# A three-FFN network in split fp32: operand tiles and weights at varied SBUF places, and two other orders of the matmuls

## The chip, the cores and the metric

One Trainium2 chip, one core. The metric is device time in microseconds (us) of one execution of the whole program; lower is better.

## The reference

A sequence of 512 tokens of width 1024 goes through three layers, each a mixer and a gated FFN with a width-3 causal convolution:

```python
x = x + rms_norm(mix, g);  u = h @ w_up                    # 1024 -> 2*4096
u = conv_b + sum(conv_w[j] * u_pad[:, j:j + S] for j in range(3))
gate, val = jnp.split(u, 2, axis=-1)
x = x + rms_norm((gelu(gate) * val) @ w_down, g)           # 4096 -> 1024
...
def conv_ffn(h, w_in, conv_w, conv_b, w_out):              # twice, 1024 -> 2*2816 -> 1024
    u = h @ w_in
    ...
    g, v = jnp.split(u, 2, axis=-1)
    return (jax.nn.silu(g) * v) @ w_out
```

The mixers are, in turn, sliding-window attention with an RWKV-7 time mix, forgetting with differential attention, and a top-k sparse attention with stick-breaking attention. All inputs and outputs are fp32.

## The kernel before, in words

**Layout.** Activations stand transposed: 128 rows of one 128-wide slice of the width, 512 tokens along the free axis, 2048 B a tile. A product in fp32 is made of three fp32r products: an operand x is split into `hi` (x rounded to fp32r) and `lo` (the rest), a weight likewise into `wh` and `wl`, and `denses` (L213 to L224) adds wh\*hi (L222), wh\*lo (L223) and wl\*hi (L224) into one PSUM bank, for each of the k-steps (128 rows of the contraction each). Every matmul loads its own 128x128 weights (LDWEIGHTS, PEld in the profile). An output slice of an up projection takes 8 k-steps, so 24 matmuls of 512 columns.

**Weights.** A `Stream` fetches units of 8 weight tiles (512 KB) from HBM by SP's DMA queue into `raw` (3 buffers, L306). `unit` (L322) copies `raw` to `wh` on ACT (L335) and subtracts on DVE to give `wl` (L336). `wh` and `wl` have 2 buffers each of 4096 B, in the pool `w`. `take` gives the next tile of the unit.

**FFN** (`ffn`, L247). After two outputs ahead (`ahead`, L233), for each of nf column blocks f it makes two outputs one after the other, gate and value: `proj` fills a bank, DVE multiplies it by the norm's factor into `u` (L265), ACT and DVE apply the convolution (L266 to L268), ACT the activation (L271), POOL the product `zu` (L273), and `split` gives `gh` and `gl` (L130, L131). There are two chunks of blocks (16 and 16 in the 1st FFN, 11 and 11 in the 2nd and 3rd). After each chunk the down projection runs over the chunk's `gh`, `gl`: 8 outputs of 16 or 11 k-steps. In the last chunk of the 1st and 3rd FFN the down projection runs in two halves of 256 columns. The PSUM banks come from `psq` (L98): two banks `q` and one `b` in turn.

**Places.** SBUF pools lie one behind the other: constants `cst`, `xp` (`x`, `hh`, `hl`, 8 tiles each, `nsq`, `bc`), `w` (`raw`, `wh`, `wl`), the later constants `cst2`, and the pool of the running phase (`gh`, `gl` and others). All tiles of `xp` and `w` are multiples of 512 B, so `hh`, `hl` and every weight tile start at the same place within 512 B (byte 224). `cst2` holds 6720 B (13\*512 + 64), so `gh` and `gl` start 64 B further on in the 1st FFN; in the 2nd and 3rd 320 B of small tiles stand ahead of them too, which puts them 128 B lower (byte 96). `hh` and `hl` are the operand tiles of all projections but the down ones.

**Order of the work.** The code emits instructions in the order in which it reads. A list scheduler then fixes the order on each engine when the program is built: at each step an engine takes the earliest emitted of those instructions that its model of the times holds to be ready, and a tile that waits for a free buffer isn't ready. On the chip each engine runs its own list in that order and waits at semaphores.

Of the kernel before, what the change touches and what calls it, by code (L numbers as in the profile page):

```python
# [10 lines left out]
F32 = mybir.dt.float32  # L11
F32R = mybir.dt.float32r
# [10 lines left out]
P = 128  # L23
S = 512
# [12 lines left out]
FFN2 = dict(nf=22, chunks=((0, 11), (11, 22)))  # L37

F1 = {"z": 4, "za": 2, "zu": 2, "u": 3, "gh": 16, "gl": 16, "acc": 8}
F2 = {"z": 4, "za": 2, "zu": 2, "u": 3, "gh": 13, "gl": 13, "acc": 8}  # L40
M2 = {"ot": 7, "cT": 4, "aq": 2, "ak": 2, "avt": 2, "p": 4, "pT": 3, "PT": 4, "on": 2, "pre": 2}
M3 = {"ot": 4, "pre": 2, "rtmp": 1, "isc": 3, "irl": 2, "selb": 3, "kf": 4, "vd": 4, "PT": 3,
      "sq": 1, "sk": 1, "svt": 2, "e": 4, "sg": 2, "sc": 2, "cq": 4, "w3": 3}

GLOBAL = {"x": 8, "hh": 8, "hl": 8, "nsq": 2, "bc": 1}

BANKS = dict(q=2, s=2, b=1, n=1, a=1, o=1)

# [17 lines left out]
class K:  # L66
    def __init__(self, tc, ctx, dbg):
        self.tc, self.nc, self.dbg = tc, tc.nc, dbg or {}
        self.c = ctx.enter_context(tc.tile_pool(name="cst", bufs=1))
        self.xp = ctx.enter_context(tc.tile_pool(name="xp", bufs=1))  # L70
        self.w = ctx.enter_context(tc.tile_pool(name="w", bufs=1))
        self.ps = ctx.enter_context(tc.tile_pool(name="ps", bufs=1, space=PSUM))
        self.dr = ctx.enter_context(tc.tile_pool(name="dr", bufs=1, space=DRAM))
        self.n = self.nq = self.nt = 0
        self.spread = False

    @contextmanager
    def phase(self, name, bufs):
# [4 lines left out]
    def slot(self, name, shape=(P, S), dt=F32, tag=None):  # L83
        self.n += 1
        tag = tag or name
        if tag in GLOBAL:
            return self.xp.tile(list(shape), dt, name=f"{name}_{self.n}", tag=tag, bufs=GLOBAL[tag])
        return self.t.tile(list(shape), dt, name=f"{name}_{self.n}", tag=tag, bufs=self.bufs.get(tag, 1))
# [124 lines left out]
    def denses(self, qs, ws, rhs, cols=(0, S)):  # L213
        nc = self.nc
        c0, c1 = cols
        n = len(rhs)
        for k, (xh, xl) in enumerate(rhs):
            xh, xl = xh[:, c0:c1], xl[:, c0:c1]
            for q, w in zip(qs, ws):
                wh, wl = w.take() if isinstance(w, Stream) else w[k]  # L220
                o = q[:, c0:c1]
                nc.tensor.matmul(o, wh, xh, start=(k == 0), stop=False)  # L222
                nc.tensor.matmul(o, wh, xl, start=False, stop=False)  # L223
                nc.tensor.matmul(o, wl, xh, start=False, stop=(k == n - 1))  # L224

    def proj(self, st, rhs):
        if st.ready:
# [19 lines left out]
    def ffn(self, x, h, up, down, cw, nf, chunks, act, done, bc=None, parts=((0, S),), mid=None, before=None, after=None):  # L247
        nc = self.nc
        if bc is None:
            self.ahead(up, h, CFG["fa"])  # L250
            bc = self.rstd(x)
        acc = {}
        for ci, (f0, f1) in enumerate(chunks):
            if ci and mid:
                mid()
            g = []
            for f in range(f0, f1):
                z = []
                for part in range(2):
                    q = self.proj(up, h)  # L260
                    c = part * nf + f
                    col = lambda j: self.pv[:, cw + j * 2 * nf + c:cw + j * 2 * nf + c + 1]
                    y = self.slot("z")
                    v = self.slot("u")
                    nc.vector.tensor_tensor(v, q, bc, op=OP.mult)  # L265
                    nc.scalar.activation(y, v, AF.Identity, bias=col(3), scale=col(2))  # L266
                    nc.vector.scalar_tensor_tensor(y[:, 1:], v[:, :S - 1], col(1), y[:, 1:], op0=OP.mult, op1=OP.add)
                    nc.vector.scalar_tensor_tensor(y[:, 2:], v[:, :S - 2], col(0), y[:, 2:], op0=OP.mult, op1=OP.add)  # L268
                    z.append(y)
                a = self.slot("za")  # L270
                nc.scalar.activation(a, z[0], act)  # L271
                u = self.slot("zu")
                nc.gpsimd.tensor_tensor(u, a, z[1], op=OP.mult)  # L273
                g.append(self.split(u, "g"))
            if ci == len(chunks) - 1:
                i0 = down.i
                for i, cols in enumerate(parts):
                    if before:
                        before(i)
                    down.i = i0  # L280
                    for m in range(8):
                        q = self.psq()
                        self.denses([q], [down], g, cols)
                        done(m, q[:, cols[0]:cols[1]], acc[m][:, cols[0]:cols[1]], cols)
                    if after:
                        after(i, cols)
                break
            for m in range(8):
                q = self.psq()
                self.dense(q, down, g)  # L290
                if ci == 0:
                    acc[m] = self.slot("acc")
                    nc.scalar.activation(acc[m], q, AF.Copy)
                else:
                    nc.vector.tensor_tensor(acc[m], acc[m], q, op=OP.add)


class Stream:
# [23 lines left out]
    def unit(self, tags=None):  # L322
        k, nc = self.k, self.k.nc
        if self.raw is None:
            self.fetch()
        raw, self.raw = self.raw, None
        if tags:
            hi, lo = ([k.slot("xw", (P, 4, P), F32R, tag=t) for t in ts] for ts in (tags[:2], tags[2:]))
        else:
            hi = [k.w.tile([P, 8, P], F32R, name=f"wh_{k.n}", tag="wh", bufs=2)]  # L330
            lo = [k.w.tile([P, 8, P], F32R, name=f"wl_{k.n}", tag="wl", bufs=2)]
        n = 8 // len(hi)
        for i, (a, b) in enumerate(zip(hi, lo)):
            part = raw[:, i * n:(i + 1) * n]
            nc.scalar.activation(a, part, AF.Copy)  # L335
            (nc.gpsimd if self.pool > 0 else nc.vector).tensor_tensor(b, part, a.bitcast(F32), op=OP.subtract)  # L336
        self.pool -= 1
        return hi, lo
# [577 lines left out]
def rope_tables(k, I, tag):  # L916
    nc = k.nc
    k.caus = k.const("caus", I["c_caus"])
    k.causb = k.c.tile([P, P], BF16, name="causb")
    nc.vector.tensor_copy(k.causb, k.caus)  # L920
    k.tri = k.const("tri", I["c_tri"])
    k.strictb = k.c.tile([P, P], BF16, name="strictb")
    nc.vector.tensor_copy(k.strictb, k.const("strict", I["c_strict"]))
    pi, ang, n, t = (k.slot(name, dt=dt, tag=tag) for name, dt in (("pi", I32), ("ang", F32), ("nn", F32), ("rt", F32)))
    nc.sync.dma_start(pi, I["positions"].partition_broadcast(P))
    inv = k.const("invf", I["c_freq"])
    nc.vector.tensor_copy(ang, pi)
    nc.vector.tensor_scalar(ang, ang, inv[:, 0:1], None, op0=OP.mult)
    nc.vector.tensor_scalar(n, ang, 1.0 / (2 * math.pi), 12582912.0, op0=OP.mult, op1=OP.add)
    nc.vector.tensor_scalar(n, n, 12582912.0, None, op0=OP.subtract)  # L930
    for c in _two_pi():
        nc.vector.scalar_tensor_tensor(ang, n, -c, ang, op0=OP.mult, op1=OP.add)
    nc.vector.tensor_scalar(ang, ang, math.pi, -math.pi, op0=OP.min, op1=OP.max)
    k.cos, k.sin = k.c.tile([P, S], F32, name="cosT"), k.c.tile([P, S], F32, name="sinT")
    nc.scalar.activation(k.sin, ang, AF.Sin, scale=inv[:, 1:2])
    nc.scalar.activation(t, ang, AF.Abs)
    half = k.c.tile([P, 1], F32, name="halfpi")
    nc.gpsimd.memset(half, math.pi / 2)
    nc.scalar.activation(k.cos, t, AF.Sin, scale=-1.0, bias=half)
    k.rot = k.const("rot", I["c_rot"])  # L940


def _two_pi():
# [434 lines left out]
        f()  # L1378


@with_exitstack
def net(ctx, tc, I, out, dbg=None, stages=(1, 2, 3)):
    nc = tc.nc
    k = K(tc, ctx, dbg)
# [4 lines left out]
    nc.gpsimd.memset(k.ones, 1.0)  # L1389
    k.identb = k.c.tile([P, P], BF16, name="identb")  # L1390
    nc.vector.tensor_copy(k.identb, k.ident)
    if 1 in stages:
        x, h, st, bc, q = first_block(k, I, ctx)
    else:
# [6 lines left out]
    if 2 in stages:  # L1401
        with k.phase("m2", M2):
            even_layer(k, I, x, h, st, bc, q)
        with k.phase("f2", F2):
            ffn2(k, I, x, 0)
    if 3 in stages:
        with k.phase("m3", M3):
            odd_layer(k, I, x)
        with k.phase("f3", F2):
            ffn2(k, I, x, 1, out)  # L1410
    else:
        with k.phase("end", {"y": 3}):
            for m in range(8):
                nc.sync.dma_start(out[:, m], x[m])
# [144 lines left out]
```

## Time and profile before

| what | us |
|---|---|
| time, median of 2 runs (2328.59 to 2328.67) | 2328.63 |
| span of the profiled execution, first to last instruction | 2314.8 |
| time outside that span (difference of the two) | 13.8 |
| PE busy in the span | 2250.8 |
| DVE busy | 1429.2 |
| ACT busy | 924.8 |
| 1st FFN, up and down | 435 to 944 |
| 2nd FFN | 1260 to 1625 |
| 3rd FFN | 1934 to 2302 |

The FFN lines are times from the span's start, read off the matmuls of their projections. PE's busy time is that of modelled, pipelined matmuls that overlap one another (one lasts 0.39 us and the next starts after some 0.23), so the rate of the work is read from the starts of the matmuls and not from their lengths.

### The profile page before, as it was taken

To read this page: it belongs to the slowest core of one execution; us is meant where nothing else is said; L and a number is where in the kernel's file an instruction comes from. 1 tells how busy PE (TensorE), PEld (TensorE's weight loads), DVE (VectorE), ACT (ScalarE), POOL (GpSimd) and SP (SyncE) were. 2 spreads that over 40 slices of the span, in tenths; PEclk is the share of its full clock that TensorE was granted. 3 is DMA by queue.
4 is the path that set the end of the run, shared out by engine and by line. 5 is a ranking of instruction groups with operands and counts; after the bars stand their busy time and mean duration, and the time that the engine had idled before them with its cause. 6 is when DMAs were issued, how large, how long until landed. Compare 5 with 4: busy or idle time off the path is not lost.

```text
span 2314.8 us, 30327 instructions
## 1 busy us (share of the span) xinstructions
PE 2250.8 (97%) x11784; PEld 1768.7 (76%) x11784; DVE 1429.2 (62%) x2597; ACT 924.8 (40%) x1533; POOL 342.9 (15%) x325
## 2 busy tenths in 40 slices
PE   8899998999999999999999999999999999999998
PEld 6677677888888889966668888888656558888888
DVE  5978765766336666643675762664795656643665
ACT  4234433544334444333344442443243344433443
POOL 2111103311001113200011111111011201111111
PEclk9999998999999999999999999999999999999999
DMA  5111121233323245311112232323211102332334
GB/s 165 59 37 35 28 63 62 69 101 100 102 94 101 91 127 169 112 33 37 55 55 83 91 100 91 101 92 99 74 46 46 46 19 91 100 100 91 101 113 152
DMA packets 66305, 192.85 MB, mean 83 GB/s; under 512 B 15808, under 2 KB 19152, under 8 KB 66160
## 3 DMA queue, kind: packets, MB, share of 16 engines
q1 hardware_dynamic: 65584, 189.70, 26.1%
q0 software_dynamic: 576, 1.19, 0.3%
q8 instruction: 93, 1.52, 0.3%
q14 instruction: 52, 0.43, 0.1%
HBM read 188.24 MB, written 2.63 MB: 82 GB/s over the span
## 4 chain that ended last, share of the span: by engine, by line
PE 85%; DVE 9%; issue 2%; ACT 2%; POOL 2%; DMA 0%; SPq 0%; DVEq 0%; ACTq 0%; POOLq 0%
PE q L222 15%; PE q L224 15%; PE q L223 15%; PE b L222 7%; PE b L224 7%; PE b L223 7%; PE o L1011 2%; DVE wl L336 1%; DVE invm L650 1%; PE s L1326 1%; PE s L1129 1%; PE s L1168 1%; DVE sc L1307 1%; PE a L813 1%; POOL nsq L163 1%
## 5 line engine op out<-in xcount | busy, mean ns | idle before, releaser
L336 DVE TENSOR_TENSOR wl<-raw,wh 128x1024 fp32r<-128x1024 f32 x341 | 433.7, 1272 | 264.8 <-ACT wh L335 263.3
L335 ACT ACTIVATE wh<-raw 128x1024 fp32r<-128x1024 f32 x341 | 359.7, 1055 | 460.2 <-PE q L223 247.7
L222 PE MATMUL q<-hh,wh 128*128 128x512 f32 (+1 forms) x1294 | 511.3, 396 | 10.1 <-ACT hh L190 7.8
L224 PE MATMUL q<-hh,wl 128*128 128x512 f32 (+1 forms) x1294 | 511.1, 395 | 0.6 <-DVE wl L336 0.6
L223 PE MATMUL q<-hl,wh 128*128 128x512 f32 (+1 forms) x1294 | 509.2, 394 | 0.6 <-DVE hl L191 0.5
L222 PEld LDWEIGHTS q<-hh,wh 128*128 128x128 f32 x1294 | 246.2, 191 | 61.6 <-ACT hh L190 7.8
L223 PEld LDWEIGHTS q<-hl,wh 128*128 128x128 f32 x1294 | 246.3, 190 | 52.3 <-issue 5.4
L224 PEld LDWEIGHTS q<-hh,wl 128*128 128x128 f32 x1294 | 245.9, 190 | 52.3 <-issue 4.5
L223 PE MATMUL b<-hl,wh 128*128 128x512 f32 (+1 forms) x602 | 233.8, 388 | 0.0
L224 PE MATMUL b<-hh,wl 128*128 128x512 f32 (+1 forms) x602 | 231.9, 385 | 0.0
L222 PE MATMUL b<-hh,wh 128*128 128x512 f32 (+1 forms) x602 | 231.6, 385 | 0.0
L273 POOL TENSOR_TENSOR zu<-za,z 128x512 f32<-128x512 f32 x76 | 100.6, 1324 | 816.5 <-DVE z L268 759.7
L224 PE MATMUL q<-gh,wl 128*128 128x256 f32 (+1 forms) x559 | 189.5, 339 | 2.2 <-DVE wl L336 2.2
L222 PE MATMUL q<-gh,wh 128*128 128x256 f32 (+1 forms) x559 | 189.4, 339 | 1.7 <-ACT gh L130 1.0
L223 PE MATMUL q<-gl,wh 128*128 128x256 f32 (+1 forms) x559 | 188.5, 338 | 0.0
L130 ACT ACTIVATE gh<-zu 128x512 fp32r<-128x512 f32 x76 | 48.1, 632 | 250.6 <-POOL zu L273 250.5
L131 DVE TENSOR_TENSOR gl<-zu,gh 128x512 fp32r<-128x512 f32 x76 | 52.6, 692 | 150.9 <-ACT gh L130 150.7
L266 ACT ACTIVATE z<-u,pv 128x512 f32<-128x512 f32 x152 | 122.7, 810 | 31.2 <-DVE u L265 31.2
L163 POOL TENSOR_TENSOR nsq<-nsq,nsq 128x256 f32<-128x256 f32 (+1 forms) x84 | 96.7, 1153 | 245.1 <-ACT nsq L158 244.8
L223 PEld LDWEIGHTS b<-hl,wh 128*128 128x128 f32 x602 | 113.9, 189 | 23.3 <-issue 2.2
L224 PEld LDWEIGHTS b<-hh,wl 128*128 128x128 f32 x602 | 113.9, 189 | 23.1 <-issue 1.7
L222 PEld LDWEIGHTS b<-hh,wh 128*128 128x128 f32 x602 | 113.9, 189 | 22.3 <-issue 0.9
(554 smaller groups left out, 3455.0 us busy)
## 6 DMA issues: line engine op xcount, KB each, us to landing
raw<-in_ffn_up SPq DMA_DIRECT2D x88, 512.0 KB, 3.6
raw<-in_w_ffn_up SPq DMA_DIRECT2D x64, 512.0 KB, 3.6
raw<-in_ffn_down SPq DMA_DIRECT2D x55, 512.0 KB, 3.6
raw<-in_w_ffn_down SPq DMA_DIRECT2D x48, 512.0 KB, 3.6
raw<-in_ev_w_in SPq DMA_DIRECT2D x24, 512.0 KB, 3.6
raw<-in_w_in SPq DMA_DIRECT2D x20, 512.0 KB, 3.8
raw<-in_od_w_in SPq DMA_DIRECT2D x20, 512.0 KB, 3.6
x<-in_x SPq DMA_DIRECT2D x16, 256.0 KB, 4.1
```

Source lines behind the costliest of these rows:

```text
L130: nc.scalar.activation(hi, x, AF.Copy)
L131: nc.vector.tensor_tensor(lo, x, hi.bitcast(F32), op=OP.subtract)
L163: (nc.gpsimd if m % chains == 0 else nc.vector).tensor_tensor(acc, acc, sq, op=OP.add)
L222: nc.tensor.matmul(o, wh, xh, start=(k == 0), stop=False)
L223: nc.tensor.matmul(o, wh, xl, start=False, stop=False)
L224: nc.tensor.matmul(o, wl, xh, start=False, stop=(k == n - 1))
L266: nc.scalar.activation(y, v, AF.Identity, bias=col(3), scale=col(2))
L273: nc.gpsimd.tensor_tensor(u, a, z[1], op=OP.mult)
L335: nc.scalar.activation(a, part, AF.Copy)
L336: (nc.gpsimd if self.pool > 0 else nc.vector).tensor_tensor(b, part, a.bitcast(F32), op=OP.subtract)
L650: nc.vector.transpose(out=M[32 * g:32 * g + 32], in_=R[j]["aab"][32 * g:32 * g + 32, :, 32 * i:32 * i + 32] .rearrange("r u c -> r c u")[: ...
L1011: k.nc.tensor.matmul(o[64 * hh:64 * hh + 64, kb * P:], v(kb, hh), pts[hh][:, 4 * kb:3 * kb + NB].rearrange("p c t -> p (c t)"), start=(kb ...
```

## The change

`hh` and `hl` become eight tiles of 2304 B each, used in turn, with the operand at an offset of its own in each (`STARTS`, in bytes). `wh` and `wl` become two tiles of 4224 B with an offset for the even and the odd unit (`WSTARTS`). Two fillers and a smaller DMA scratch put the pools `xp`, `w` and the phase pool of the FFNs at multiples of 512 B. In the 2nd FFN the three products of a k-step run in the order wh\*hi, wl\*hi, wh\*lo. In the 3rd FFN gate and value of a block are made together: their matmuls alternate between two banks, and the weights have 3 buffers `wph`, `wpl` each in the phase pool, for the down projection of that FFN too.

```diff
-F2 = {"z": 4, "za": 2, "zu": 2, "u": 3, "gh": 13, "gl": 13, "acc": 8}
+F2 = {"wph": 3, "wpl": 3, "z": 4, "za": 2, "zu": 2, "u": 3, "gh": 13, "gl": 13, "acc": 8}
...
+STARTS = {"hh": (0, 16, 32, 48, 64, 128, 256, 192), "hl": (0, 0, 0, 0, 32, 32, 16, 16)}
+WSTARTS = ((0, 32), (0, 16))
...
     def slot(self, name, shape=(P, S), dt=F32, tag=None):
...
+        if tag in STARTS:
+            i = self.turn[tag] = (self.turn.get(tag, -1) + 1) % 8
+            t = self.xp.tile([P, 576], dt, name=f"{name}_{self.n}", tag=f"{tag}{i}")
+            return t[:, STARTS[tag][i] // 4:STARTS[tag][i] // 4 + S]
...
+        if self.paired and len(qs) == 2:
+            for k, (xh, xl) in enumerate(rhs):
+                us = [w[k] for w in ws]
+                for i, (a, x) in enumerate(((0, xh), (1, xh), (0, xl))):
+                    for q, u in zip(qs, us):
+                        nc.tensor.matmul(q[:, c0:c1], u[a], x[:, c0:c1], start=(k == 0 and i == 0), stop=(k == n - 1 and i == 2))
+            return
...
                 nc.tensor.matmul(o, wh, xh, start=(k == 0), stop=False)
-                nc.tensor.matmul(o, wh, xl, start=False, stop=False)
-                nc.tensor.matmul(o, wl, xh, start=False, stop=(k == n - 1))
+                for a, x, last in ((wl, xh, 0), (wh, xl, 1)) if self.swapped else ((wh, xl, 0), (wl, xh, 1)):
+                    nc.tensor.matmul(o, a, x, start=False, stop=(last == 1 and k == n - 1))
...
+                if self.paired:
+                    pair = up.ready[:2]
+                    del up.ready[:2]
+                    if not pair:
+                        pair = [self.psq(), self.psq()]
+                        self.denses(pair, [[up.take() for _ in range(8)] for _ in range(2)], h)
                 for part in range(2):
-                    q = self.proj(up, h)
+                    q = pair[part] if self.paired else self.proj(up, h)
...
-        if tags:
+        if k.paired:
+            hi, lo = ([k.slot(n, (P, 8, P), F32R)] for n in ("wph", "wpl"))
+        elif tags:
...
-            hi = [k.w.tile([P, 8, P], F32R, name=f"wh_{k.n}", tag="wh", bufs=2)]
-            lo = [k.w.tile([P, 8, P], F32R, name=f"wl_{k.n}", tag="wl", bufs=2)]
+            k.turn["w"] = i = 1 - k.turn.get("w", 1)
+            hi, lo = ([k.w.tile([P, 1056], F32R, name=f"{n}_{k.n}", tag=f"{n}{i}")[:, o[i] // 4:o[i] // 4 + 1024].rearrange("p (a b) -> p a b", b=P)]
+                      for n, o in zip(("wh", "wl"), WSTARTS))
...
+def filler(k, size):
+    k.n += 1
+    t = k.c.tile([P, size // 4], F32, name=f"filler_{k.n}")
+    k.nc.gpsimd.memset(t[:, 0:1], 0.0)
```

The fillers are called with 1824 (in `net`, ahead of the first block) and 1472 (at the end of `rope_tables`); `net` sets `k.swapped` around the 2nd FFN and `k.paired` from the 3rd on; the program is built with `dynamic_dma_scratch_size=8192`.

## Rows read from the trace of the kernel before

**Rows 1.** The page, part 1 and the clock line of part 2.

```profile
PE 2250.8 (97%) x11784; PEld 1768.7 (76%) x11784; DVE 1429.2 (62%) x2597; ACT 924.8 (40%) x1533; POOL 342.9 (15%) x325
...
PEclk9999998999999999999999999999999999999999
```

**Rows 2.** The page, part 4: the chain that ended last, by engine.

```profile
PE 85%; DVE 9%; issue 2%; ACT 2%; POOL 2%; DMA 0%; SPq 0%; DVEq 0%; ACTq 0%; POOLq 0%
```

**Rows 3.** Groups by line and shape, PE: count, busy us, mean ns, idle before.

```profile
L222 PE MATMUL q<-hh,wh 128*128 128x512 f32 x1240 | 494.3, 399 | 7.8 <-ACT hh L190 7.8
...
L222 PE MATMUL b<-hh,wh 128*128 128x512 f32 x560 | 219.1, 391 | 0.0
...
L222 PE MATMUL q<-gh,wh 128*128 128x512 f32 x278 | 109.7, 395 | 0.0
...
L222 PE MATMUL b<-gh,wh 128*128 128x512 f32 x114 | 45.0, 395 | 0.0
...
L222 PE MATMUL o<-hh,wh 128*128 128x512 f32 x24 | 9.7, 403 | 0.0
```

**Rows 4.** Timeline of PE, 2nd FFN, up projection: start us, duration us.

```profile
1500.83 0.39 PE L223 MATMUL q<-hl,wh 128*128 128x512 f32 x1
...
1502.19 0.39 PE L223 MATMUL q<-hl,wh 128*128 128x512 f32 x1
```

**Rows 5.** Timeline of PE, 1st FFN, down projection.

```profile
599.65 0.39 PE L222 MATMUL b<-gh,wh 128*128 128x512 f32 x1
...
601.71 0.39 PE L222 MATMUL b<-gh,wh 128*128 128x512 f32 x1
```

**Rows 6.** Timeline of PE, 2nd FFN, down projection.

```profile
1403.78 0.39 PE L223 MATMUL b<-gl,wh 128*128 128x512 f32 x1
1404.01 0.40 PE L224 MATMUL b<-gh,wl 128*128 128x512 f32 x1
1404.25 0.39 PE L222 MATMUL b<-gh,wh 128*128 128x512 f32 x1
...
1405.88 0.40 PE L223 MATMUL q<-gl,wh 128*128 128x512 f32 x1
```

**Rows 7.** Timeline of PE, 1st FFN, from down back to up projection.

```profile
670.14 0.39 PE L224 MATMUL b<-gh,wl 128*128 128x512 f32 x1
670.37 0.40 PE L222 MATMUL q<-hh,wh 128*128 128x512 f32 x1
...
672.69 0.39 PE L223 MATMUL q<-hl,wh 128*128 128x512 f32 x1
672.92 0.39 PE L224 MATMUL q<-hh,wl 128*128 128x512 f32 x1
```

**Rows 8.** Timeline of PE, 3rd FFN, where one bank follows another.

```profile
2149.57 0.39 PE L223 MATMUL q<-hl,wh 128*128 128x512 f32 x1
2149.79 0.39 PE L224 MATMUL q<-hh,wl 128*128 128x512 f32 x1
2150.02 0.39 PE L222 MATMUL b<-hh,wh 128*128 128x512 f32 x1
2150.25 0.39 PE L223 MATMUL b<-hl,wh 128*128 128x512 f32 x1
```

**Rows 9.** Timeline of all engines there: the weights' split and the evacuation.

```profile
2149.99 1.06 ACT L335 ACTIVATE wh<-raw 128x1024 fp32r<-128x1024 f32 x1 [0.36 <-PE q L223]
...
2150.22 0.69 DVE L265 TENSOR_TENSOR u<-q,bc 128x512 f32<-128x512 f32 x1 [1.31 <-PE q L224]
...
2151.09 1.23 DVE L336 TENSOR_TENSOR wl<-raw,wh 128x1024 fp32r<-128x1024 f32 x1 [0.17 <-ACT wh L335]
```

**Rows 10.** Timeline of PE, 3rd mixer, last blocks of the attention.

```profile
1899.58 0.60 PE L999 MATMUL n<-ident,e 128*128 128x128 f32 x4
1899.94 0.48 PE L222 MATMUL q<-hh,wh 128*128 128x512 f32 x1
1900.25 0.40 PE L223 MATMUL q<-hl,wh 128*128 128x512 f32 x1
1900.49 0.65 PE L999 MATMUL a<-ident,e 128*128 128x128 f32 x4
```

**Rows 11.** Waits of PE: total us, times, longest us.

```profile
PE q L222 <- ACT hh L190: 7.8, 1, 7.8
...
PE q L224 <- DVE wl L336: 2.8, 5, 1.1
```

**Rows 12.** Stretches of the 3rd FFN (second up part, 256-wide down part): length, busy us (instructions) by engine, clock.

```profile
2119.00:2236.00 117.00, 117.00 (x518) 96.89 (x517) 75.65 (x95) 49.81 (x62) 14.78 (x12) 1.00 0.31 96
2237.00:2302.00 65.00, 63.92 (x535) 63.48 (x535) 39.93 (x61) 28.65 (x38) 15.25 (x13) 1.00 0.53 164
```

More of the change, by code (lines that the diff above doesn't have):

```diff
@@ L74, in __init__ @@
         self.n = self.nq = self.nt = 0
-        self.spread = False
+        self.turn = {}
+        self.spread = self.paired = self.swapped = False
     @contextmanager
@@ L940, in rope_tables @@
     k.rot = k.const("rot", I["c_rot"])
+    filler(k, 1472)
 def _two_pi():
@@ L1391, in net @@
     nc.vector.tensor_copy(k.identb, k.ident)
+    filler(k, 1824)
     if 1 in stages:
@@ L1404, in net @@
         with k.phase("f2", F2):
+            k.swapped = True
             ffn2(k, I, x, 0)
+            k.swapped = False
     if 3 in stages:
@@ L1409, in net @@
         with k.phase("f3", F2):
+            k.paired = True
             ffn2(k, I, x, 1, out)
@@ L1549 @@
     arrays = layout(inputs)
-    nc = bacc.Bacc("TRN2", target_bir_lowering=False, num_devices=1)
+    nc = bacc.Bacc("TRN2", target_bir_lowering=False, num_devices=1, dynamic_dma_scratch_size=8192)
     I = {n: nc.dram_tensor(f"in_{n}", v.shape, mybir.dt.from_np(v.dtype), kind="ExternalInput").ap()
```

## The prediction

> **What bounds the kernel now.** I read the page first: PE is busy for 97% of the span at the full clock nearly throughout [rows 1], and the chain that ended last is 85% PE [rows 2]. PE waits little (its longest wait is 7.8 us, at the start; those of the q banks for `wl` come to 2.8 us) [rows 11]. So the time is the number of matmuls times the distance between their starts, and that distance is what the change can touch. Three fp32r products a k-step make 3 x (1240 + 560 + 24) = 5472 matmuls of 512 columns on `hh`/`hl` and 3 x (278 + 114) = 1176 on `gh`/`gl` [rows 3].
>
> Next I read the distance from the timeline of PE, stage by stage. In an up projection six distances take 1502.19 - 1500.83 = 1.36 us: 226.7 ns each [rows 4]. The clock is at 2.4 GHz there, at which 512 columns take 213.3 ns, so 13.3 ns (32 cycles) are lost on each matmul. In the down projection of the 1st FFN nine take 2.06 us, 228.9 ns [rows 5], in that of the 2nd nine take 2.10 us, 233.3 ns, alternately about 0.23 and 0.24 [rows 6]. Line, shape and engine state are the same in all three; what differs is where the streamed operand lies in SBUF against the weights that are loaded meanwhile: 0, +64 and -128 B within 512 B. After a change from one place to the other the distance doesn't settle at once: the eleven from 670.37 to 672.92 take 2.55 us, 231.8 ns, with hh against weights at 0 B, where the settled distance is 226.7 [rows 7]. So the loss depends on the relative place and on what came just before.
>
> **The change part by part.**
>
> *Places.* It adds no instruction to this loop; it changes the distances. By the tile sizes the weights now start at bytes 0 and 128 (wh, wl of even units) and 288 and 400 (odd units) within 512, hh at 0, 16, 32, 48, 64, 128, 256, 192 and hl at 256, 272 or 288. The relative place thus differs from one matmul to the next, which the trace of before doesn't show; bounds come from the rows. Below, 213.3 ns, the columns alone. Above, 240 ns, the longer of the two that alternate (1404.01 to 1404.25) [rows 6]. For 5472 matmuls that is from -73 to +73 us. The nearest rows are the three settled places, whose mean is 229.6, and the unsettled stretch, 231.8. I take 230, close to the settled mean since the 3rd FFN keeps one operand for four matmuls: +3.3 ns x 5472 = +18.1 us. For gh and gl, 8 x 16 x 3 = 384 in the 1st FFN and 1176 - 384 = 792 in the others go to the same 230: +1.1 x 384 = +0.4 and -3.3 x 792 = -2.6 us. The 256-wide matmuls (535 in 65 us in one of the two stretches, waits included: 121 ns [rows 12]) I leave where they are; 1 ns on each would be about 1.3 us. The whole of +18.1 counts, although some of these matmuls lie in the mixers beside other waits.
>
> The Trainium skill (SBUF — State Buffer, "SBUF: two separate sides" and "A bandwidth-pool intuition that's wrong") gives PE its own ports, which wait on no other engine, and a second independent read port for LDWEIGHTS. By that the place would cost nothing and the sum would be without this term; the rows differ, 226.7 against 233.3 ns for the same instructions. The same skill (TensorE: Matmul & The Clock Gate, "Wait — 56ns, not 53.3ns?") states 215.7 ns from start to start at 512 columns; no row here reaches it, and if all 5472 did, the sum would be some 60 us lower (an estimate from that page).
>
> *The tiles themselves.* Eight tags in turn instead of eight buffers: all users take tiles in eights and in the same order, so nothing waits that did not. Two more memsets on POOL, which is 15% busy [rows 1]: 0. The list of each engine is drawn up anew, so mixers may shift; I give them 0, with 5 us to either side, below PE's one long wait [rows 11].
>
> *Order in the 2nd FFN.* Same instructions. wl is needed one matmul (0.23 us) earlier, wh is free one later. A unit lasts 24 x 0.227 = 5.4 us; the split of the unit after next starts 0.03 us after the last reader of wh ends (2149.57 + 0.39 to 2149.99) and takes 1.06, then 1.23 us, until 2152.32 [rows 9]: some 3 us to spare. Cost 0. Without that cover it would be 0.23 x 44 units = 10 us.
>
> *Pairs in the 3rd FFN.* A pair needs two units at once, and three buffers hold one more than the pair in work. So the second unit of the next pair can be split only when this pair's last-but-one matmul has read wh. Let it start at T. It ends at T + 0.39, the copy on ACT runs from T + 0.42 to T + 1.48, and its first reader, due at T + 3 x 0.227 = 0.68, starts after its weight load (0.19 us) at about T + 1.70: 1.0 us late. wl runs from T + 1.52 to T + 2.75; its reader, by then due at T + 2.15, starts at T + 2.97: 0.8 us more. If DVE first takes both banks' evacuation (0.69 us each [rows 9], from T + 0.65), it is 1.3. That makes 1.8 to 2.3 us a pair if PE runs the matmuls as written. It recurs in 9 pairs of chunk 0 (f = 2 to 10) and 10 of chunk 1 (f = 12 to 21): 35 to 44 us. What hides it: the built order takes on each engine what is ready. The rows show it: two matmuls of the output projection, written after the last attention block, stand between that block's transposes [rows 10]. While the second unit is missing, 24 matmuls of the first bank have their weights, 5.4 us against 2.3. The second bank, the previous pair's first, is evacuated by T + 1.34 to 2.0 and is hidden by the same. Residue: what the builder's times are off by, 0 to 0.3 us a pair by the 2.8 us of such waits in the whole run [rows 11]; I take 0.15 x 19 = 3 us. DVE and ACT have room for the burst of two evacuations (75.7 and 49.8 of 117 us) [rows 12]. Two banks in turn gain nothing in themselves: where b follows q the distance stays 0.23 [rows 8].
>
> *Sum.* 18.1 + 0.4 - 2.6 + 3 = +18.9 us on the profiled span of 2314.8: 2333.7. The runs take 13.8 us more than that span, 2328.6 against 2314.8; with these the time is 2347.5.
>
> **The rivals.**
>
> *Place doesn't matter,* and the three distances come from something else in the stages, by the rule of separate ports above. For it: hh and hl take turns in the up projection and give the same 226.7 [rows 4]. Against it: in the down projections of the 1st and 2nd FFN the instructions are the same and only the place differs [rows 5, 6]. Time: 2328.6 + 3 = 2331.6.
>
> *Some places lose nothing.* The 32 cycles vanish where operand and weights don't meet. For it: one of the three places is already 6.6 ns better than another [rows 4, 6], so the loss isn't fixed. Against it: none of the three settled places has it, and the one in use is the best of them. With a quarter of the matmuls at 213.3 and the rest at 230 the mean is 225.8: -0.9 x 5472 - 3.1 x 384 - 7.5 x 792 + 3 = -9 us, 2319. With half, 221.7: -27.4 - 2.8 - 9.2 + 3 = -36 us, 2292. Faster by over 2% needs more than half.
>
> *Pairs stall as written* (the other side). PE meets the second unit's missing weights in each of the 19 pairs, because the builder's model holds the split to be faster than it is, or keeps the alternation. Price 35 to 44 us on top of the places' 15.9: 2380 to 2389. It becomes slower than 2% from 1.6 us a pair. For it: ACT's wait for the last reader of wh is in the trace already [rows 9]. Against it: rows 10 and 11.
>
> *All places bad.* 240 ns everywhere: +73 + 11.1 x 384/1000 + 6.7 x 792/1000 + 3 = +86 us, 2414. For it: each change of place brings longer distances first [rows 7]. Against it: those come to 231.8, not 240.
>
> **How the numbers follow.** Forecast 0.50 (2335 to 2365), place doesn't matter 0.16, places that lose nothing 0.17 (0.06 of it beyond 2%), pairs stall 0.13, all places bad 0.04. Over 2%, about what a measurement of this kernel can tell from no change, means below 2282 or above 2375. Faster 0.06; slower 0.13 + 0.04 less a little for stalls that are partly hidden, 0.15; within 2% 0.79. The range leaves out a tenth at each end: 2300, between a quarter and a half of free places, to 2386, inside the stalled pairs.
>
> **What would show it.** Right: in the timelines of the up projections distances that no longer repeat every three matmuls, scattered between 0.22 and 0.24 with a mean near 230; in the 3rd FFN matmuls of one bank ahead of the other at the start of each pair, and waits of PE for `wpl` and `wph` below 6 us in sum. Wrong: a mean below 226 or above 235 (places mis-sized), a settled 226.7 everywhere (place irrelevant), or waits on `wpl`, `wph` of 1 us and more, 19 times.

## The result and the profile after

| | before | after |
|---|---|---|
| time, median, us | 2328.63 | 2357.57 (2 runs: 2351.37, 2363.76) |
| ratio, 95% interval | | 1.0112 [1.0077, 1.0148] |
| span of the profiled execution, us | 2314.8 | 2349.4 |
| mean granted clock in it | 0.989 | 0.986 |

The change makes the kernel 28.9 us slower; 18.9 were forecast. The time lies inside the range and within 2% of before.

The page after, parts 1, 2 (clock) and 4, is the one of before [rows 1, 2] with a longer PE: the same 11784 matmuls, shares within one per cent of before, 33 us more in PE.

```profile
PE 2283.7 (97%) x11784; PEld 1774.2 (76%) x11784; DVE 1422.4 (61%) x2597; ACT 923.7 (39%) x1533; POOL 359.1 (15%) x327
...
PEclk9989998999999999999999999999999999999999
...
PE 85%; DVE 9%; issue 2%; POOL 2%; ACT 2%; DMA 0%; SPq 0%; DVEq 0%; ACTq 0%; POOLq 0%
```

The groups of PE by line and shape after, which answer to [rows 3]:

```profile
L237 PE MATMUL q<-hh,wh 128*128 128x512 f32 x1016 | 412.4, 406 | 7.9 <-ACT hh L198 7.9
...
L230 PE MATMUL q<-hh,wph 128*128 128x512 f32 x216 | 82.0, 396 | 0.5 <-ACT wph L359 0.5
...
L230 PE MATMUL b<-hh,wph 128*128 128x512 f32 x120 | 47.4, 395 | 0.0
```

L237 and L239 are the old L222 to L224; L230 are the pairs of the 3rd FFN, with weights `wph`, `wpl`. A matmul lasts 0.40 us as before; these modelled durations don't show the loss. It stands in the starts. The timeline of PE after, in three stretches (1st FFN up, 2nd FFN up, start of a pair in the 3rd FFN):

```profile
499.66 0.40 PE L239 MATMUL b<-hh,wl 128*128 128x512 f32 x1
499.90 0.40 PE L237 MATMUL b<-hh,wh 128*128 128x512 f32 x1
500.13 0.39 PE L239 MATMUL b<-hl,wh 128*128 128x512 f32 x1
500.36 0.40 PE L239 MATMUL b<-hh,wl 128*128 128x512 f32 x1
...
505.50 0.40 PE L237 MATMUL q<-hh,wh 128*128 128x512 f32 x1
...
1329.71 0.39 PE L237 MATMUL b<-hh,wh 128*128 128x512 f32 x1
...
1335.51 0.39 PE L239 MATMUL q<-hh,wl 128*128 128x512 f32 x1
...
2040.62 0.40 PE L230 MATMUL q<-hl,wph 128*128 128x512 f32 x1
...
2041.33 0.42 PE L230 MATMUL b<-hh,wph 128*128 128x512 f32 x1
2041.58 0.39 PE L230 MATMUL q<-hl,wph 128*128 128x512 f32 x1
...
2042.73 0.39 PE L230 MATMUL b<-hh,wpl 128*128 128x512 f32 x1
```

From 499.66 to 505.50 there are 25 distances: 5.84 / 25 = 233.6 ns. From 1329.71 to 1335.51 there are 25 again: 232.0 ns. Before, it was 226.7 in the 2nd FFN [rows 4] and 226.8 on average in both, at a granted clock of 1.00 as here. In the last stretch the first bank's matmuls (`q`) run ahead and the second bank (`b`) gets one now and then, until its weights are there.

The waits of PE in the 3rd FFN after (total us, times, longest us):

```profile
PE q L237 <- ACT gh L138: 3.3, 2, 2.5
...
PE q L230 <- ACT wph L359: 0.5, 1, 0.5
PE q L239 <- DVE wpl L360: 0.3, 1, 0.3
```

The pairs wait 0.5 + 0.3 = 0.8 us for weights in the whole stage, not 19 times 1.8 us. New is a wait of 2.5 us for `gh`, near the start of the down projection's halves, where a matmul needs the last block's `gh`. Before, the wait for it was

```profile
PE q L222 <- ACT gh L130: 1.0, 1, 1.0
```

`gh` is made from the product `zu` on POOL. Gate and value of the last block are now evacuated together, so `zu` starts 5.2 us after the first matmul of the halves (3.9 before), and it takes 3.19 us (1.28 before). After the change it starts while DVE is making two splits, and ends 1.1 us after the second; before, it started ahead of DVE's split, and the split took longer. The rows, after and then before, with the window that follows the wait after (the clock is the last column but two):

```profile
2273.70 2.35 DVE L360 TENSOR_TENSOR wpl<-raw,wph 128x1024 fp32r<-128x1024 f32 x2
2273.98 3.19 POOL L294 TENSOR_TENSOR zu<-za,z 128x512 f32<-128x512 f32 x1 [9.06 <-ACT za L292]
...
2278.00:2281.00 3.00, 3.00 (x15) 3.00 (x16) 0.55 (x1) 0.00 (x0) 0.00 (x0) 0.51 0.43 152
...
2240.97 1.28 POOL L273 TENSOR_TENSOR zu<-za,z 128x512 f32<-128x512 f32 x1 [9.60 <-DVE z L268]
2241.11 2.22 DVE L336 TENSOR_TENSOR wl<-raw,wh 128x1024 fp32r<-128x1024 f32 x1 [0.31 <-ACT wh L335]
```

The wait has a second price: after it the granted clock is 0.51 for 3 us (the lower level, 1.2 GHz), and some 16 of the 256-wide matmuls start 213 ns apart in place of 118. That is 1.5 us.

Where the time came from, by mean distance between the starts of neighbouring matmuls (distances under 262 ns, or 135 ns for 256 columns; the longer ones are counted as waits, those at the lower clock among them):

| matmuls | count | before, ns | after, ns | us |
|---|---|---|---|---|
| 1st FFN up | 1416 | 226.8 | 232.7 | +8.4 |
| 2nd FFN up | 1056 | 226.8 | 231.8 | +5.3 |
| 3rd FFN up | 1056 | 226.8 | 232.0 | +5.5 |
| mixers, `hh`/`hl` | 1944 | 228.2 to 229.0 | 231.8 to 232.3 | +6.9 |
| down, 512 wide, 1st / 2nd / 3rd FFN | 384 / 528 / 264 | 228.9 / 233.3 / 233.3 | 231.1 / 232.9 / 228.9 | +0.8 -0.2 -1.2 |
| down, 256 wide, 1st / 3rd FFN | 768 / 528 | 117.8 / 118.8 | 118.9 / 117.7 | +0.9 -0.6 |
| 3rd FFN, waits and gaps (up, down 512, halves) | | | | +0.7 +1.0 +3.5 |

The sum is 31 us. The span grew by 34.6; the other 3 to 4 us lie in the first mixer, where the granted clock was lower in this execution (0.950 on average from 0 to 450 us, against 0.959 before).

### The profile page after: what moved, and what is told of

Same layout as the page of the kernel before. It is cut to its first block, busy times and chain, and to the rows that moved or that the text cites. A ratio compares the mean times of both kernels' runs of the same rounds, so it can differ in the third digit from the quotient of the medians.

```text
span 2349.4 us, 30360 instructions
## 1 busy us (share of the span) xinstructions
PE 2283.7 (97%) x11784; PEld 1774.2 (76%) x11784; DVE 1422.4 (61%) x2597; ACT 923.7 (39%) x1533; POOL 359.1 (15%) x327
## 4 chain that ended last, share of the span: by engine, by line
PE 85%; DVE 9%; issue 2%; POOL 2%; ACT 2%; DMA 0%; SPq 0%; DVEq 0%; ACTq 0%; POOLq 0%
PE q L239 27%; PE q L237 13%; PE b L239 12%; PE q L230 6%; PE b L237 6%; PE b L230 3%; PE o L1036 2%; DVE wl L360 1%; PE s L1351 1%; PE s L1154 1%; DVE invm L674 1%; PE s L1193 1%; DVE sc L1332 1%; PE a L837 1%; PE a L1024 1%
## 5 line engine op out<-in xcount | busy, mean ns | idle before, releaser
L360 DVE TENSOR_TENSOR wl<-raw,wh 128x1024 fp32r<-128x1024 f32 x264 | 336.4, 1275 | 202.3 <-ACT wh L359 201.4
L359 ACT ACTIVATE wh<-raw 128x1024 fp32r<-128x1024 f32 x264 | 278.9, 1057 | 415.8 <-PE q L239 233.8
L237 PE MATMUL q<-hh,wh 128*128 128x512 f32 (+1 forms) x1070 | 429.1, 401 | 10.3 <-ACT hh L198 7.9
L239 PE MATMUL q<-hl,wh 128*128 128x512 f32 (+1 forms) x1070 | 428.1, 400 | 0.6 <-DVE hl L199 0.5
L239 PE MATMUL q<-hh,wl 128*128 128x512 f32 (+1 forms) x1070 | 428.5, 401 | 0.0
L237 PEld LDWEIGHTS q<-hh,wh 128*128 128x128 f32 x1070 | 204.8, 192 | 58.2 <-ACT hh L198 7.9
L239 PEld LDWEIGHTS q<-hl,wh 128*128 128x128 f32 x1070 | 205.2, 192 | 48.9 <-issue 6.3
L239 PEld LDWEIGHTS q<-hh,wl 128*128 128x128 f32 x1070 | 205.0, 192 | 45.7 <-issue 4.2
L239 PE MATMUL b<-hl,wh 128*128 128x512 f32 (+1 forms) x474 | 185.6, 392 | 0.0
L239 PE MATMUL b<-hh,wl 128*128 128x512 f32 (+1 forms) x474 | 184.1, 388 | 0.0
L237 PE MATMUL b<-hh,wh 128*128 128x512 f32 (+1 forms) x474 | 183.7, 387 | 0.0
L239 PE MATMUL q<-gh,wl 128*128 128x512 f32 (+1 forms) x372 | 129.8, 349 | 2.1 <-DVE wl L360 2.1
L360 DVE TENSOR_TENSOR wpl<-raw,wph 128x1024 fp32r<-128x1024 f32 x77 | 94.9, 1234 | 58.5 <-ACT wph L359 58.4
L237 PE MATMUL q<-gh,wh 128*128 128x512 f32 (+1 forms) x372 | 129.3, 348 | 0.8 <-ACT wh L359 0.8
L239 PE MATMUL q<-gl,wh 128*128 128x512 f32 (+1 forms) x372 | 129.8, 349 | 0.0
L359 ACT ACTIVATE wph<-raw 128x1024 fp32r<-128x1024 f32 x77 | 81.1, 1055 | 122.6 <-PE q L230 39.8
```

Source lines behind the costliest of these rows:

```text
L239: nc.tensor.matmul(o, a, x, start=False, stop=(last == 1 and k == n - 1))
```

## The experiments

Three theories were put against each other: the places alone make the loss; the two orders do, above all the pairs; the eight tags in turn do, whatever their offsets. They were run in three groups, each beside the kernel before on the same chip; its medians there were 2327.06 (25 runs), 2330.57 (9) and 2327.57 (17).

**Places alone.** The changed kernel without the two orders:

```diff
-            k.swapped = True
...
-            k.paired = True
```

> The varied places alone, both orders as before. If the places make the whole difference: 2347 to 2353 us, distances of 231.5 to 233 ns in all three up projections, and in the 3rd FFN no waits for a pair's weights. If the orders carry a part of it (rival): more than 8 us below the changed kernel's 2351, with the 2nd and 3rd FFN's up projections nearer to 227 than the 1st's.

Measured: 2354.96 us, ratio 1.0107 [1.0079, 1.0135]; the up projections take 232.68, 232.75 and 232.75 ns. The time is 2 us above the range expected, the distances are inside theirs. The timeline of PE in the 3rd FFN, 25 distances in 5.80 us, 232.0 ns:

```profile
1999.77 0.39 PE L239 MATMUL q<-hh,wl 128*128 128x512 f32 x1
...
2005.57 0.40 PE L237 MATMUL q<-hh,wh 128*128 128x512 f32 x1
```

The whole slowdown is there without the orders. Against the changed kernel the 2nd FFN shows that the order wh\*hi, wl\*hi, wh\*lo is 0.9 ns better at these places (231.82), 1 us in all.

**Orders alone.** Eight tags in turn and both orders, but every operand and weight at byte 0:

```diff
-STARTS = {"hh": (0, 16, 32, 48, 64, 128, 256, 192), "hl": (0, 0, 0, 0, 32, 32, 16, 16)}
-WSTARTS = ((0, 32), (0, 16))
+STARTS = ("hh", "hl")
+WSTARTS = ((0, 0), (0, 0))
...
-            t = self.xp.tile([P, 576], dt, name=f"{name}_{self.n}", tag=f"{tag}{i}")
-            return t[:, STARTS[tag][i] // 4:STARTS[tag][i] // 4 + S]
+            return self.xp.tile([P, S], dt, name=f"{name}_{self.n}", tag=f"{tag}{i}")
```

> Both orders of the change, but hh, hl and all weights at one place (byte 0 within 512; gh, gl at 0 in the 1st FFN and 320 in the others). If only places count: 226.7 ns in all up projections, the down ones no worse than before, waits for the pairs' weights of 2 to 6 us in sum, so 2324 to 2331 us. If alternating banks or the other order shorten a matmul: below 226 in the 3rd or 2nd FFN. If the pairs stall as written: 35 us above before.

Measured: 2335.15 us, ratio 1.0023 [0.9996, 1.0049], no difference that can be told; up 226.73 and 226.77 ns in the 1st and 2nd FFN, so the swapped order and the eight tags cost nothing. The time is 4 us above the range expected, and PE waited 1.0 us for the pairs' weights where 2 to 6 were expected. The mean granted clock of these eight runs was 0.981 (0.983 in the 25 of before beside them), which by the slope given further down is worth some 3 us. In the 3rd FFN the pairs cost what the next kernel, without them, doesn't have: 244.7 us for the up projection against 241.9, and more waits. The waits of PE in the 3rd FFN with the pairs:

```profile
PE q L236 <- ACT gh L137: 3.3, 2, 2.5
...
PE q L229 <- ACT wph L358: 0.7, 1, 0.7
PE q L238 <- DVE wpl L359: 0.3, 1, 0.3
```

and without them, in the next kernel:

```profile
PE q L236 <- ACT gh L137: 1.0, 1, 1.0
```

The waits explain 1.0 us of the 2.8 in the up projection. Another 0.8 is in the neighbouring distances (227.50 against 226.75 ns, 1031 of them), and the rest in 18 small gaps of 0.06 us, as the timeline of the kernel with the orders alone shows one:

```profile
2003.34 0.39 PE L229 MATMUL q<-hh,wpl 128*128 128x512 f32 x1
2003.56 0.45 PE L229 MATMUL q<-hh,wph 128*128 128x512 f32 x1
2003.85 0.39 PE L229 MATMUL q<-hl,wph 128*128 128x512 f32 x1
...
2004.98 0.40 PE L229 MATMUL q<-hh,wpl 128*128 128x512 f32 x1
2005.22 0.40 PE L229 MATMUL q<-hl,wph 128*128 128x512 f32 x1
2005.45 0.40 PE L229 MATMUL q<-hh,wph 128*128 128x512 f32 x1
```

The matmul at 2003.56 is held for some 0.06 us (0.29 to the next start in place of 0.23). From 2003.85 to 2005.45 seven distances then take 1.60 us, 228.6 ns each, where 226.7 is the settled value. The first five still have it (four or five in every case); then up to ten distances scatter between 224 and 241 ns before the rate settles again. The same follows each of the 18 gaps, so the gap is taken for its cause.

**Everything at one place, no orders.** As before it, without the two orders, and with a tile of 192 B in the phase pools of the 2nd and 3rd FFN that brings `gh` and `gl` to byte 0 too:

```diff
+    pad = k.slot("pad", (P, 48))
+    nc.gpsimd.memset(pad[:, 0:1], 0.0)
```

> No other order, and every operand and weight tile at one place, gh and gl too. If the settled distance is a matter of relative place alone: 226.7 ns in the down projections also, which saves 384 x 2.2 ns + 792 x 6.6 ns = 6 us, so 2320 to 2325 us, below the kernel before. If the down projections' longer distance has another cause: 2328.

Measured: 2324.11 us, ratio 0.9979 [0.9957, 1.0001]. All up and down projections of 512 columns stand at 226.67 to 226.75 ns. The timeline of PE in the down projection of the 3rd FFN, 25 distances of 226.4 on average where before had 233.3 [rows 6]:

```profile
2089.82 0.39 PE L238 MATMUL b<-gl,wh 128*128 128x512 f32 x1
...
2095.48 0.39 PE L238 MATMUL q<-gh,wl 128*128 128x512 f32 x1
```

But the 256-wide matmuls went from 117.8 to 119.9 ns, which takes some 2 us back (2.1 x 768 + 1.2 x 528 ns): 0 B is not their best place.

**One place for each stage.** Four kernels give `hh` and `hl` one offset for each of the nine projections, weights at 0, no orders, so that each place can settle (the tiles are larger and the fillers smaller to match, not shown; this is the first of the four):

```diff
+STARTS = {"hh": (64, 0, 16, 128, 0, 32, 192, 0, 48)}
+STARTS["hl"] = STARTS["hh"]
+WSTARTS = ((0, 0), (0, 0))
...
+            j = self.turn[tag] = self.turn.get(tag, -1) + 1
+            i, o = j % 8, STARTS[tag][j // 8] // 4
```

> One place for each stage, weights at 0: hh and hl at 16 B in the 1st FFN, 32 in the 2nd, 48 in the 3rd (64, 128, 192 in the mixers), orders as before. If it is the change of place from matmul to matmul that costs: each stage settles into a pattern that repeats every few matmuls, and the three means lie apart within 226 to 234, not all near 232. If single places are bad in themselves, above all those off the 64 B grid: 232 or more in all three.

> One place for each stage again, weights at 0: 128 B in the 1st FFN, 256 in the 2nd, 192 in the 3rd (320, 384, 448 in the mixers). If the distance depends on the relative place within 256 B (64 and 320 gave the same 228.9, and 384 gave 233.3): 233.3 in the 1st FFN, alternating; 226.7 in the 2nd; another repeating pattern in the 3rd. If it depends on it within 512 B: 256 B gives something else than 226.7.

> One place for each stage, weights at 0: 96 B in the 1st FFN, 160 in the 2nd, 224 in the 3rd (80, 112, 144 in the mixers). By the places measured so far: repeating patterns between 226.7 and 234. A place that reads without loss would show 213 to 216 ns; my theory has no place for that, a model of two reads that collide in one part of the memory would.

> One place for each stage, weights at 0: 8 B in the 1st FFN, 240 in the 2nd, 12 in the 3rd (176, 208, 4 in the mixers). By the places measured so far 0 B is the best and its neighbours are worse, so repeating patterns of 228 to 234 ns; if the grid is one of 16 B, 8 and 12 B come out like 0 or like 16 (226.7 or 231.7). Any value below 226 would mean that a better place exists between the sampled ones.

Their times, one run each, are 2351.79, 2345.12, 2360.66 and 2358.07 us. What they are for is the settled distance by place (operand's start less weights' start, modulo 256 B):

| bytes | 0 | 4 | 8 | 12 | 16 | 32 | 48 | 64 | 80 | 96 |
|---|---|---|---|---|---|---|---|---|---|---|
| ns | 226.7 | 236.6 | 233.3 | 228.9 | 231.7 | 233.3 | 230.0 | 228.9 | 231.1 | 233.3 |

| bytes | 112 | 128 | 144 | 160 | 176 | 192 | 208 | 224 | 240 |
|---|---|---|---|---|---|---|---|---|---|
| ns | 231.1 | 233.3 | 233.3 | 234.3 | 233.4 | 233.3 | 230.0 | 233.3 | 236.7 |

Timeline of PE with 16 B (1st FFN), 25 distances in 5.79 us, 231.6 ns, and with 48 B (3rd FFN), 25 in 5.75, 230.0:

```profile
499.72 0.40 PE L241 MATMUL q<-hl,wh 128*128 128x512 f32 x1
...
505.51 0.39 PE L241 MATMUL q<-hh,wl 128*128 128x512 f32 x1
...
1999.84 0.39 PE L241 MATMUL q<-hh,wl 128*128 128x512 f32 x1
...
2005.59 0.39 PE L239 MATMUL q<-hh,wh 128*128 128x512 f32 x1
```

With 256 B (2nd FFN of the second kernel), 25 in 5.67, 226.8: the same as 0.

```profile
1329.83 0.39 PE L239 MATMUL q<-hh,wh 128*128 128x512 f32 x1
...
1335.50 0.39 PE L241 MATMUL b<-hl,wh 128*128 128x512 f32 x1
```

With 240 B (2nd FFN of the fourth), 24 in 5.68, 236.7:

```profile
1329.75 0.40 PE L239 MATMUL b<-hh,wh 128*128 128x512 f32 x1
...
1335.43 0.40 PE L239 MATMUL q<-hh,wh 128*128 128x512 f32 x1
```

Same line, shape, bank turn and granted clock (1.00); only the place differs, and the distance by 10 ns between these two. The expectation that 8 and 12 B go with their neighbours 0 and 16 missed, and 4, 160 and 240 B lie above the 234 expected. No place falls below 226.7, and the mean of the 19 is 232.2.

The place alone doesn't fix the settled distance to the nanosecond. In the 2nd FFN of the fourth kernel the down projection of the first chunk stands at 228.9, and that of the second chunk at 233.3 throughout, with `gh`, `gl` at the same 64 B and the granted clock at 1.00. 25 distances of each take 5.72 and 5.83 us:

```profile
1420.05 0.39 PE L241 MATMUL q<-gl,wh 128*128 128x512 f32 x1
...
1425.77 0.39 PE L241 MATMUL q<-gh,wl 128*128 128x512 f32 x1
...
1609.92 0.40 PE L241 MATMUL q<-gh,wl 128*128 128x512 f32 x1
...
1615.75 0.40 PE L239 MATMUL q<-gh,wh 128*128 128x512 f32 x1
```

In the other kernels with `gh` at 64 B against the weights all these stretches settle at 228.9, so this is one in some twenty. At 0 B the FFN stages of every kernel settle at 226.7. Differences of a few ns between single entries of the table should be read with that in mind.

**Does the changing cost, beside the places?** Offsets changed from tile to tile in multiples of 64 B, no orders:

```diff
+STARTS = {"hh": (0, 64, 128, 192, 256, 320, 384, 448), "hl": (256, 0, 320, 64, 384, 128, 448, 192)}
+WSTARTS = ((0, 0), (0, 0))
```

> Places that change from matmul to matmul, but only by multiples of 64 B, weights at 0. If a change of place costs in itself (the reads never settle): about 232 ns, no repeating pattern of a few matmuls, 2345 to 2352 us. If each matmul has the distance of its own place: the mean of the settled ones, 226.7, 228.9, 233.3 and that of 192 B, about 230, so 2338 to 2343 us.

Measured: 2348.52 us, ratio 1.0074 [1.0047, 1.0101]; up 231.9 ns, unsettled throughout. The four settled places that it visits (226.7, 228.9, 233.3, 233.3) average 230.6: changing costs some 1.3 ns a matmul more.

**Weights alone varied,** operands all at byte 0, `WSTARTS` as in the change:

> Only the weights at varied places (0, 128, 288, 400 B), hh and hl all at 0. If the relative place counts: wh and wl in turn change it at every matmul, as much as moving the operands does, so 231 to 233 ns in the up projections. If only the operand's own place counts: 226.7.

Measured: 2349.37 us (one run), up 231.1 to 231.2 ns. It is enough to move the weights: the operand's own place is not what counts. That the relative place does fits the kernel before, where both lie at byte 224, and the aligned one, where both lie at 0: 226.7 in both.

**Changes of 256 B.** `hh` and `hl` alternate between bytes 0 and 256, weights at 0:

```diff
+STARTS = {"hh": (0, 256, 0, 256, 0, 256, 0, 256), "hl": (256, 0, 256, 0, 256, 0, 256, 0)}
+WSTARTS = ((0, 0), (0, 0))
```

> hh and hl take turns between 0 and 256 B within 512, weights at 0. If only the place within 256 B counts, also when it changes: 226.7 ns in all up projections, settled, and no loss for the eight tags as such, so a span within the spread of the aligned kernel's. If a change of place costs whatever the places are: about 232.

Measured: 2323.65 us (one run); up 226.8 ns in all three FFNs and settled. In the timeline of PE ten distances take 2.27 us, 227 ns:

```profile
1329.69 0.39 PE L237 MATMUL q<-hh,wh 128*128 128x512 f32 x1
...
1331.96 0.39 PE L239 MATMUL q<-hl,wh 128*128 128x512 f32 x1
```

Tiles that change places cost nothing as long as the place modulo 256 B stays.

**The best of both.** Everything at one place, and the weights 192 B higher while the 256-wide halves run, which puts the operand at 64 B modulo 256:

```diff
+                self.woff = 48 if len(parts) > 1 else 0
...
+            hi, lo = ([k.w.tile([P, 1088], F32R, name=f"{n}_{k.n}", tag=f"{n}{i}")[:, k.woff:k.woff + 1024].rearrange("p (a b) -> p a b", b=P)]
```

> Everything at one place within 256 B, orders as before, but for the 256-wide halves of the down projections the weights lie 64 B lower, so that the operand is at +64 to them. Down projections 226.7 ns (512 wide), and 117.4 to 117.8 instead of 119.9 ns (256 wide). Sum of the terms against before: 0.9 + 5.3 + 0.6 = 7 us less, a ratio of about 0.997.

Measured: 2326.83 us, ratio 0.9988 [0.9967, 1.0008]: not told apart from before. The distances came as expected (512 wide 226.7 everywhere, 256 wide 117.7 and 117.8). Its granted clock was lower: 0.979 in the profiled execution. The windows from 300 to 350 us, in the first mixer, show where (the clock is the last column but two), for the kernel before

```profile
300.00:350.00 50.00, 48.23 (x439) 37.95 (x439) 30.32 (x110) 18.45 (x38) 1.52 (x2) 1.00 0.28 80
```

and for this one

```profile
300.00:350.00 50.00, 47.67 (x278) 36.42 (x278) 29.73 (x103) 11.56 (x22) 1.47 (x2) 0.69 0.16 47
```

At 0.69 PE does 278 matmuls there in place of 439 (in the 50 us that follow it does 414 in place of 289, so part of this is a shift in time). Its three runs at a mean clock of 0.987 took 2314.27, 2314.9 and 2316.55 us, against 2320.62 to 2323.03 of before at 0.987 to 0.988: some 6 us better at equal clock. Within each kernel of this study the time falls by about 1.66 us for 0.001 more of mean clock. A straight line of time against clock gives, at 0.985, 2319 us for these 12 runs and 2326 for the 17 of before beside them: the 7 us that the terms sum to. Whether the lower clock is this kernel's or chance stays open, so its time isn't shown to beat that of the kernel before.

Nor is 64 B the best place for 256-wide matmuls. In the 2nd mixer of the third single-place kernel, with `hh` and `hl` at 112 B against `wh` and `wl`, they settle at 113.3 ns, 27 distances in 3.06 us, at a granted clock of 1.00; with everything at 0 B the same stretch settles at 120.0:

```profile
987.72 0.28 PE L239 MATMUL b<-hh,wh 128*128 128x256 f32 x1
...
990.78 0.28 PE L239 MATMUL b<-hh,wh 128*128 128x256 f32 x1
```

No kernel tried 112 B in the halves of the down projections.

## Why the prediction was right, and where its sizes were off

*PE bounds the time, and the change acts by the places.* Right. Places alone give 1.0107, orders alone 1.0023. The rival that place doesn't matter falls by the single-place kernels, 226.7 against 236.7 ns for the same instructions. The Trainium skill (SBUF — State Buffer, "A bandwidth-pool intuition that's wrong (but worth ruling out)") gives LDWEIGHTS a second, independent read port; as far as that would make the place free, these 10 ns speak against it.

*The value of 230 ns.* This is the step that was mis-sized: +18.1 us forecast; measured +26.1 (the first four lines of the table), as the mean is 232 and not 230. That is 8 of the 12 us between the 31 of the table and the 18.9 of the sum. The value came from the mean of three settled places, of which 0 and 64 B are two of the best three of the 19 now known, and the reason given for staying near it, one operand for four matmuls in the 3rd FFN, didn't help: that stage has 232.0 as the others. The unsettled stretch of [rows 7], 231.8 ns, was the nearer row, since the change never lets a place settle; 232 from it, 5.3 ns more than 226.7 on 5472 matmuls, gives +29. That is a little too much because the mixers started from 228 to 229 and not from 226.7.

*gh and gl.* Forecast +0.4 and -2.6; measured +0.8 and -1.4. The 3rd FFN gains more than forecast (228.9, a settled value: its weights lie in tiles of the phase pool that all start at one place), the 2nd almost nothing (232.9). The 256-wide matmuls: forecast 0, measured +0.9 and -0.6, each within the 1.3 us named.

*Order of the 2nd FFN: 0.* Right: 226.77 ns with it at one place against 226.72 without. Its gain of 1 us at varied places had not been foreseen.

*Pairs: 3 us.* The mechanism held: `b` runs behind `q` at the start of a pair, as the built order has it, and PE waits 0.8 us for weights, below the 6 us named as the bound. The rival of pairs that stall as written falls. The size was 5.2 us, of which 3.5 are at the halves. The prediction priced the burst of two evacuations at nothing because DVE and ACT have room on average. At the end of the chunk it isn't hidden: the product on POOL starts later and takes 3.19 us beside DVE's splits, PE waits about 2.0 us longer in all, and the lower clock behind the wait costs 1.5. The prediction has no term for either. The pairs aren't the only way to it: in three kernels without them (the first and third of the single-place ones and that with multiples of 64 B) DVE's split starts just ahead of the product, which then takes 2.3 us; PE waits 2.3 us for `gh`, and the clock falls likewise. In the seven other changed kernels without pairs, as before, the product starts first and takes 1.3. So how much of the 3.5 belongs to the pairs isn't separated. With everything at one place the pairs cost about 2 us more in the up projection (2.8 for 0.7), by the gaps and what they unsettle.

*Time outside the span: 13.8 us.* This was no fixed overhead. In the runs of this study time and span differ by 1.7 to 3.3 us. The profiled execution of before had a mean clock of 0.989; the runs of before in this study average 0.983. The 13.8 stood in for that lower clock; it is on both sides of the forecast difference and doesn't change it.

*Some places lose nothing.* Falls: none of 19 places is below 226.7 ns. The Trainium skill's 215.7 ns (TensorE: Matmul & The Clock Gate, "Wait — 56ns, not 53.3ns?") is not reached by any settled stretch here. *All places bad,* 240 ns everywhere, falls too; 236.7 is the worst place.

## What to carry to other kernels

Where each 512-wide fp32r matmul loads its own 128x128 weights, start the streamed operand and the weights at the same byte modulo 256 (for 256-wide ones another place was better here), and read the rate from the starts of the matmuls, stage by stage, since busy times don't show it. If places change from matmul to matmul, price them with an unsettled stretch of the trace and not with settled ones. Before making two outputs together, look at the end of the last block, where both are evacuated at once and the next stage waits for them, and at which engine starts first there; a wait of 2.5 us of PE cost another 1.5 by the clock behind it.

## What the runs showed of the hardware that was not expected

- The distance depends on the relative place to within 4 bytes: 226.7, 236.6, 233.3 and 228.9 ns for 0, 4, 8 and 12 B. One place, 64 B, settled at 228.9 and once at 233.3.
- The settled distances of most places are whole numbers of 8 cycles at 2.4 GHz: 226.67 ns are 544, 230.0 are 552, 233.33 are 560, 236.67 are 568; with 16 B four matmuls, repeating 228, 234, 235 and 230 ns, take 2224.
- After a gap of 0.06 us four or five distances keep the settled value, and then up to ten scatter between 224 and 241 ns.
- 256-wide matmuls have other good places: 117.7 ns at 64 B and 113.3 at 112 B, against 119.9 at 0 B.
- POOL's product took 1.28 us where it began ahead of DVE's split of the weights, which then took 2.2, and 2.3 to 3.2 us where DVE began first, by as little as 0.01 us. After PE's waits of 2.3 to 2.5 us behind that the granted clock stood at its lower level for some 3 us; after those of 1.0 us it stayed at 1.00.

Why the place matters is open. That two reads of SBUF by PE, operand and weights, meet in the same cycles would fit the places, but it is only argued, and it doesn't say why one place settled at two values; nor is it known why changing places adds some 1.3 ns to the mean of the places.
